# A 16-row, 512-byte write to the output ahead of all else in an interleaving copy

## Chip, cores and metric

The kernel runs on one core of a Trainium2 chip. The metric is the device time of one execution in microseconds (us); lower is better. Before the change three runs gave a median of 317.45 us (317.14 to 317.56). A difference counts as faster or slower here when it is over 2%, which is 6.3 us.

A ratio in this text is the mean time of one kernel's runs over the mean time of the other's runs of the same rounds. It is not quite the ratio of the medians that stand beside it.

## The reference

Two float32 arrays of 32 x 256 x 1024 (33.5 MB each) are interleaved element by element.

```python
def reference(x, y):
    batch, seq, dim = x.shape
    result = np.zeros((batch, seq, dim * 2), dtype=np.float32)
    result[..., 0::2] = x
    result[..., 1::2] = y
    return result.astype(np.float32)
```

Nothing is computed. 67.1 MB have to come in and 67.1 MB have to go out.

## The kernel before

The arrays are cut into eight blocks of 128 rows x 8192 elements. Loads are issued from the sync engine (the profile calls their queue q1). The vector engine (DVE) copies x to the even and y to the odd places of an output tile, in two halves for each block. Stores are issued from the scalar engine (queue q10). All tiles have two buffers.

```python
    WL = 8192
    WS = 4096
    ...
    xpool = ctx.enter_context(tc.tile_pool(name="xp", bufs=2))
    ypool = ctx.enter_context(tc.tile_pool(name="yp", bufs=2))
    opool = ctx.enter_context(tc.tile_pool(name="op", bufs=2))
    ...
    for lw in lwidths:                       # eight blocks
        ...
        nc.sync.dma_start(out=xtile, in_=xs)
        nc.sync.dma_start(out=ytile, in_=ys)
        soff = 0
        while soff < lw:                     # two halves
            ...
            nc.vector.tensor_copy(out=otile[:, 0::2], in_=xsub)
            nc.vector.tensor_copy(out=otile[:, 1::2], in_=ysub)
            nc.scalar.dma_start(out=os_, in_=otile)
            soff += width
        start += P * lw
```

## Time and profile before

| what | value | where it is read |
|---|---|---|
| time, median of 3 | 317.45 us | runs |
| span of the profiled execution | 315.0 us | first line of the page |
| last packet ends | 313.79 us | packet records of the trace |

A load or store of 4 MB is cut into 128 packets of 32 KB, eight for each of the 16 DMA engines. A packet normally takes 1.213 us. The prediction shows the lines of the page and how they are read.

### The profile page before, as it was taken

The numbers are of one execution on the slowest core, as the hardware profiler recorded it, in microseconds if no ns is written. First come the engines' busy times: TensorE is split into PE (matmuls) and PEld (weight loads), VectorE is DVE, ScalarE is ACT, GpSimd is POOL, SyncE is SP. The second block draws the span as 40 slices with busy tenths as digits, with TensorE's granted clock in tenths as the row PEclk, the third lists the DMA queues.
The fourth block names the chain that finished last, engine by engine and source line by source line (L and its number), as shares of the span: only waits on it lengthen the run. The fifth ranks groups of instructions, "written<-read, shape, count | busy, mean of one in ns | idle before, by whom it ended". The sixth has DMA issues, their size and how long they took to land.

```text
span 315.0 us, 148 instructions
## 1 busy us (share of the span) xinstructions
DVE 72.6 (23%) x32; POOL 0.2 (0%) x4
## 2 busy tenths in 40 slices
DVE  0334002214022230322204131040410505005500
POOL 0000000000000000000000000000000000000000
DMA  8999999999999999999999999999999999999997
GB/s 333 408 458 387 412 454 412 454 412 454 412 454 412 458 408 458 408 458 408 458 408 458 424 441 424 441 429 437 429 437 429 437 429 437 433 433 437 429 437 304
DMA packets 4608, 134.22 MB, mean 426 GB/s; under 512 B 512, under 2 KB 512, under 8 KB 512
## 3 DMA queue, kind: packets, MB, share of 16 engines
q1 hardware_dynamic: 2304, 67.11, 49.8%
q10 hardware_dynamic: 2304, 67.11, 49.3%
HBM read 67.11 MB, written 67.11 MB: 426 GB/s over the span
## 4 chain that ended last, share of the span: by engine, by line
DMA 83%; DVE 11%; DVEq 1%; issue 0%; SPq 0%
DMA out_dram<-otile 76%; DMA ytile<-in_y_dram 7%; DVE otile L64 6%; DVE otile L63 5%; DVEq L95 1%; SPq L49 0%; DVEq L63 0%
## 5 line engine op out<-in xcount | busy, mean ns | idle before, releaser
L63 DVE COPY otile<-xtile 128x4096 f32<-128x4096 f32 x16 | 36.6, 2294 | 197.9 <-DMA out_dram<-otile 184.8
L64 DVE COPY otile<-ytile 128x4096 f32<-128x4096 f32 x16 | 36.6, 2292 | 28.9 <-DMA ytile<-in_y_dram 28.9
L84 POOL MEMSET const-uint8-127<- 128x1 uint8 x1 | 0.1, 103 | 0.0
L84 POOL MEMSET const-bfloat16-1.0<- 128x1 bf16 x1 | 0.1, 102 | 0.0
L84 POOL MEMSET const-float32-1.0<- 128x1 f32 x1 | 0.1, 100 | 0.0
L84 POOL MEMSET const-float32-0.0<- 128x1 f32 x1 | 0.1, 99 | 0.2 <-issue 0.2
## 6 DMA issues: line engine op xcount, KB each, us to landing
out_dram<-otile ACTq DMA_DIRECT2D x16, 4096.0 KB, 30.6
xtile<-in_x_dram SPq DMA_DIRECT2D x8, 4096.0 KB, 42.1
ytile<-in_y_dram SPq DMA_DIRECT2D x8, 4096.0 KB, 59.2
```

Source lines behind the costliest of these rows:

```text
L63: nc.vector.tensor_copy(out=otile[:, 0::2], in_=xsub)
L64: nc.vector.tensor_copy(out=otile[:, 1::2], in_=ysub)
L84: nc = _bacc.Bacc("TRN2", target_bir_lowering=False, num_devices=1)
L95: with _tile.TileContext(nc) as tc:
```

## The change

The intent seems to be to make the first write to the output early, when nothing depends on it, so that whatever a first write costs is not paid in the middle of the stream. The bytes written are zeros. The first real store overwrites them, so the result stays right.

```diff
     assert sum(lwidths) == total // P
+
+
+    wpool = ctx.enter_context(tc.tile_pool(name="wp", bufs=1))
+    zero = wpool.tile([16, 128], fp32, name="zero")
+    nc.vector.memset(zero, 0.0)
+    first = dataclasses.replace(of, offset=0, ap=[[2 * WL, 16], [1, 128]])
+    nc.scalar.dma_start(out=first, in_=zero)
 
     start = 0
     for lw in lwidths:
```

## The prediction

> **What bounds the kernel now.** I read the page first: the busy shares, the row of GB/s in slices, the DMA queues and the chain that ended last.
>
> ```profile
> span 315.0 us, 148 instructions
> ...
> DVE 72.6 (23%) x32; POOL 0.2 (0%) x4
> ...
> DMA packets 4608, 134.22 MB, mean 426 GB/s; under 512 B 512, under 2 KB 512, under 8 KB 512
> ...
> q1 hardware_dynamic: 2304, 67.11, 49.8%
> q10 hardware_dynamic: 2304, 67.11, 49.3%
> ...
> DMA 83%; DVE 11%; DVEq 1%; issue 0%; SPq 0%
> ```
>
> The reader is to see three things. The only computing engine, the vector engine, works 23% of the span. The loads (q1) and the stores (q10) move 67.11 MB each, and their packets take 49.8% + 49.3% = 99.1% of the time of the 16 DMA engines, 0.991 x 315.0 = 312.2 us. And 83% of the chain is DMA. The 11% of DVE in the chain is not a bound: other transfers run under those copies, as the windows show. Their columns are start and end, length, busy time (and count) of DVE and of POOL, granted clock, DMA share, GB/s. I cut them at multiples of 14.55 us, twelve packets of 1.213 us, because the packets of the 16 engines run nearly in step and a shorter window shows that beat and not the rate.
>
> ```profile
> 0.00:1.70 1.70, 0.00 (x0) 0.20 (x4) 1.00 0.00 0
> 1.70:16.25 14.55, 3.17 (x2) 0.00 (x0) 1.00 1.04 430
> 16.25:30.80 14.55, 5.82 (x3) 0.00 (x0) 1.00 0.98 399
> 30.80:45.35 14.55, 0.00 (x0) 0.00 (x0) 1.00 1.00 432
> ...
> 74.45:292.70 218.25, 50.03 (x22) 0.00 (x0) 1.00 1.01 434
> 292.70:307.25 14.55, 4.50 (x2) 0.00 (x0) 1.00 1.01 437
> ```
>
> Nothing moves for 1.70 us. From 30.8 us to the end the rate is level at 432 to 437 GB/s whether the vector engine works or not. So the end is set by how many bytes there are, by the 1.7 us ahead of the first packet, and by whatever slows the engines on the way. One window stands out: 16.25 to 30.80 us, where the share is full (0.98) but the rate is 399.
>
> **The dip.** I looked at the single packet records of the trace. There are 4096 data packets of 32 KB, 256 for each engine, and nearly all take 1.213 us: 256 x 1.213 = 310.5 us. The first packet starts at 1.72 us and the last ends at 313.79 us, which is 312.07 us; the packet times sum to 312.02 us for an engine. So the engines have no gap worth naming. The 1.5 us over 310.5 are in two places only. The first packet of each of the 16 engines, which all start between 1.7 and 2.4 us, takes 1.3 to 2.2 us; over 1.213 this is 0.67 us for an engine. And 25 load packets that start between 26.6 and 30.5 us take 1.3 to 2.6 us, 0.82 us for an engine. Not one packet after that is longer than 1.26 us. This second place is where the first store arrives:
>
> ```profile
> 22.76 4.50 DVE L64 COPY otile<-ytile 128x4096 f32<-128x4096 f32 x2 [5.19 <-DMA ytile<-in_y_dram]
> 25.09 2.56 ACTq L65 DMA_DIRECT2D out_dram<-otile  x2
> 27.29 0.33 SPq L50 DMA_DIRECT2D ytile<-in_y_dram  x1
> ```
>
> In this stretch of the timeline the first two stores are issued at 25.09 us and some 2.2 us later. The first packet of q10 starts at 29.8 us; the loads just ahead of it are the stretched ones. So the kernel before pays 0.82 us once, when its store queue is used for the first time. The 16 to 30 us window agrees in size: (433 - 399) / 433 x 14.55 = 1.1 us, with part of that the edge of the window. A tiny write put ahead of everything looks meant for exactly this: to pay for the first write early. That is the whole prize there is.
>
> **What the Trainium skill says.** "DMA: Bandwidth & Descriptors", section "Where 436 GB/s comes from", gives a ceiling of 435.2 GB/s for the 16 ports. The trace agrees: 434 GB/s over 218 us. This leaves nothing to win in the steady part. The same page, "Queues, rings and completion order", says that each DMA engine takes turns between the queues that have work for it, a packet at a time. The trace fits: after 29.8 us packets of q10 and q1 alternate. So the small write can't be stuck behind the 8 MB of loads that are queued by then; it waits for a packet or two. The same page, "Two DMAs through the same engine are not ordered", says that order between two transfers comes only from waiting on the first one's semaphore. The first real store writes the same bytes, so a correct program must make it wait for the small write; the kernel before has no such wait. "Latency and other measured facts" gives 0.2 us on average and 2 us under high load for an access to HBM. The 0.67 us on each engine's first packet lies between; no record of the kernel before shows a small write by itself.
>
> **The change, part by part.** It removes nothing.
> - It adds a memset of 16 x 128 on the vector engine. This engine is idle until 13.08 us, and the four memsets of 128 x 1 on POOL take 0.10 us each. My estimate is 0.1 to 0.2 us near 0.7 us, in idle time. On the path to the end: 0.
> - It adds one issue on the scalar engine's queue, which idles until 25.09 us. The issues of stores take 0.34 us. On the path: 0, unless the loads' issues at 0.73 and 1.15 us are held up behind it. The small write has to wait for the memset, so the first load should go out first.
> - It adds 16 packets of 512 bytes and 16 semaphore packets, one pair for an engine. At 434 / 16 = 27.1 GB/s an engine moves 512 bytes in 0.02 us, and semaphore packets have 9 ns in the trace. Sum: some 0.03 us for an engine, on the path, since the engines have no gap: +0.03 us.
> - It adds a wait of the first store. If the small write is issued near 1 to 1.5 us and needs two packets' turns (2 x 1.2 to 2.2 us) and a round trip of up to 2 us, it lands by some 3 to 8 us. The first store can't go before 25.09 us. The wait costs 0. Later stores wrote other bytes, and in the kernel before the second store did not wait for the overlapping range of the first, so they gain no wait.
> - It moves every later transfer one place in the rotation of eight completion semaphores. A transfer that takes up a semaphore again waits for its last user; this was eight transfers, two rounds of the loop, before. One place more at the head leaves that distance at eight. Cost 0.
> - It may move the 0.82 us of the first write from 27 us to 2 us. There each engine sits in the 0.67 us of its first read anyway, so the two can overlap. If they overlap wholly the sum is 0.03 - 0.82 = -0.79 us; if not at all it is +0.03 us.
>
> **The rivals.** (A) The stall belongs to the first use of the store queue or of the way to the output, and the small write takes it in the shadow of the first reads: 317.45 - 0.3 to 0.8, so 316.6 to 317.1 us. For it: the stall is there once, and no packet after 32 us is stretched. (B) The stall belongs to a queue that wakes up while the other one keeps the engines full, or it is moved but not hidden. Then the small write has long drained by 25 us, the queue wakes up again, and the time stays at 317.4 to 317.6. For it: after the first two stores q10 never runs dry in the kernel before, so the trace can't tell "first" from "after idling". (C) The small write brings a stall of its own, in full, with the old one left where it is: +0.7 to 0.8, so 318.2 us. Against it: 512 bytes for an engine are little to stall on. (D) The first store's new wait takes the path: it would need the small write to land after 25.09 us, and q1's turns don't allow for that. An engine that becomes the bound I can't see: DVE would have to grow fourfold.
>
> **Range and chances.** I give A 0.45, B 0.4, C 0.15: 0.45 x 316.85 + 0.4 x 317.5 + 0.15 x 318.2 = 317.3; with the full prize possible in A I say 317.2 us. The three runs before spread over 0.42 us and the profiled run took 316.73, so I allow 0.4 beyond A's middle and stop just under C: 316.4 to 318.1 us. Two per cent are 6.3 us. The largest gain is 0.8 us, and even 1.72 us of start, 0.67 and 0.82 taken away together would be 3.2 us, 1%. No path to 2% is left upwards or downwards but a thing I have not seen: faster 0.01, same 0.98, slower 0.01.
>
> **What would show it.** Right: a span of 314.2 to 315.2 us, the same level 434 GB/s from 31 us on, 4640 packets, a DVE memset near 0.7 us, a small write that lands before 10 us, and the first store issued at 24 to 25.5 us without a new wait. A is right if the window 16.25 to 30.80 rises from 399 to over 420 and no load packet near 27 us is stretched; B if it stays near 400. Wrong: the first load's issue pushed past 1.2 us, a wait for the small write ahead of a store in the list of waits, or stretched packets later on.

## The result, and the profile after

The changed kernel took 316.34 us in the median (316.18 to 316.80, 6 runs). The kernel before took 317.13 us (316.34 to 317.56, 6 runs, with the three known ones among them). The ratio is 0.998, with a 95% interval of 0.9965 to 0.9995. This is the same within 2%, with a gain of about 0.2% that the interval sets apart from zero, though only just.

The page of the changed kernel, in the lines that answer to those of before:

```profile
span 314.5 us, 152 instructions
...
DVE 72.8 (23%) x33; POOL 0.2 (0%) x4
...
DMA packets 4640, 134.23 MB, mean 427 GB/s; under 512 B 528, under 2 KB 544, under 8 KB 544
...
q1 hardware_dynamic: 2304, 67.11, 49.9%
q10 hardware_dynamic: 2336, 67.12, 49.4%
...
out_dram<-zero ACTq DMA_DIRECT2D x1, 8.0 KB, 7.1
```

The reader is to see that q10 has 32 packets more, 16 of 512 bytes and 16 for semaphores, that the engines are as full as before, and that the 8 KB of the small write took 7.1 us from issue to landing. The timeline of the changed kernel shows where it lies:

```profile
0.73 0.37 SPq L56 DMA_DIRECT2D xtile<-in_x_dram  x1
0.81 0.17 DVE L45 MEMSET zero<- 16x128 f32 x1 [0.81 <-PEq L91]
1.01 0.42 ACTq L47 DMA_DIRECT2D out_dram<-zero  x1
1.15 0.42 SPq L57 DMA_DIRECT2D ytile<-in_y_dram  x1
...
25.01 33.63 ACTq L72 DMA_DIRECT2D out_dram<-otile  x3
```

Issued at 1.01 us, it landed at 8.1 us. The first store goes out at 25.01 us (25.09 before), so its new wait for the small write, over at 8.1 us, costs nothing. The loads are issued when they were before. The windows of the changed kernel, cut as those of before (start and end, length, busy time of DVE and POOL, clock, DMA share, GB/s):

```profile
1.70:16.25 14.55, 3.28 (x2) 0.00 (x0) 1.00 1.06 433
16.25:30.80 14.55, 5.72 (x3) 0.00 (x0) 1.00 0.96 396
30.80:45.35 14.55, 0.00 (x0) 0.00 (x0) 1.00 1.00 432
```

The dip at the first store is still there: 396 GB/s, against 399 before. So the small write did not take the hold-up away. The packet records say the same of the sum: near 27 us the stretched load packets cost 0.65 us for an engine, against 0.82 before. They also show a difference that the sum hides. Before, 14 engines start their first store packet between 29.82 and 30.35 us, and two only at 31.82 us, after a load packet of 2.6 us. After, all 16 start between 29.84 and 30.17 us, and no load packet there is longer than 1.95 us.

The records do not name the engine of a packet. It is found by following the times: each packet of an engine starts 3 to 4 ns before the one ahead of it ends. Followed in this way, the two engines run 23 loads ahead of their first store, and the other 14 run 22. In this text an engine with such a load more is called a late engine. That load only changed places with a store, so 1.21 us of the delay are not lost; the rest is, and the two end 0.65 us behind the middle engine.

The kernel ends with its slowest engine: in the twelve traces of the table that ends the experiments, the measured time is 2.90 to 2.94 us more than the end of the last packet. The last packet ended at 313.79 us before and at 313.34 us after, while the middle engine (the ninth of the 16 by the end of its last packet) ended at 313.14 and 313.22 us.

One trace each is no proof, so the experiments had two questions: is the gain real and is it these late engines, and what causes the general hold-up?

### The profile page after: what moved, and what is told of

Read it like the earlier page. It is cut to its first block, busy times and chain, and to the rows that moved or that the text cites. A ratio compares the mean times of both kernels' runs of the same rounds, so it can differ in the third digit from the quotient of the medians.

```text
span 314.5 us, 152 instructions
## 1 busy us (share of the span) xinstructions
DVE 72.8 (23%) x33; POOL 0.2 (0%) x4
## 4 chain that ended last, share of the span: by engine, by line
DMA 83%; DVE 11%; DVEq 1%; issue 0%; SPq 0%
DMA out_dram<-otile 76%; DMA ytile<-in_y_dram 7%; DVE otile L71 6%; DVE otile L70 5%; DVEq L102 1%; SPq L56 0%; DVEq L70 0%
## 5 line engine op out<-in xcount | busy, mean ns | idle before, releaser
L71 DVE COPY otile<-ytile 128x4096 f32<-128x4096 f32 x16 | 36.6, 2292 | 39.8 <-DMA ytile<-in_y_dram 39.8
```

## The experiments

Twelve runs were made, all with the right result. I name the theories as the expectations do. R: the difference is chance. W: the small write shortens the hold-up. V: each engine's first write to memory is slow now and then, and an early write takes that away. Q: it is the first use of queue q10. D: the general hold-up comes each time stores arrive at engines that were full of loads. F: that hold-up comes only once.

### 1. The changed kernel again (after_again)

No edit.

> The changed kernel unchanged, to see whether its 0.2% is there again and where it comes from. Theory R (the end is set by the engine that is held up longest at the first store, and that hold-up varies from execution to execution whatever the kernel): ratio to the kernel before between 0.998 and 1.002, with single times of both kernels spread over some 316.2 to 317.6 us; 16 to 30 load packets between 26 and 31 us stretched by 0.5 to 0.9 us for an engine, as in both traces so far. Theory W (the small write shortens the hold-up): ratio 0.997 to 0.999, interval below 1, and the stretch again at 0.65 us or under.

Measured: 316.54 us (316.38 to 316.78), the kernel before 316.73 us (316.19 to 317.56, 11 runs), ratio 0.999, interval 0.9975 to 1.0005. The hold-up was 0.94 us for an engine. By itself this doesn't confirm the gain, and W falls: the general hold-up is not shorter with the small write. But the kernel before had five of its 11 times between 317.2 and 317.6, and the changed kernel had none over 316.8.

### 2. The memset without the write (memset_only)

```diff
     nc.vector.memset(zero, 0.0)
-    first = dataclasses.replace(of, offset=0, ap=[[2 * WL, 16], [1, 128]])
-    nc.scalar.dma_start(out=first, in_=zero)
```

> The small write taken out of the changed kernel, its memset left in. Theory R: no difference to the kernel before, ratio 0.999 to 1.001, stretch near 27 us of 0.5 to 0.9 us for an engine. Theory W: as the kernel before, 1.000, with a stretch at about 0.82 us, and slower than the changed kernel of the same rounds by about 0.5 us. If it is as fast as the changed kernel and both are faster than before, the gain is not of the write.

Measured: 317.17 us (316.14 to 317.60), ratio 1.0005. Four of six times are above 317.0. In its trace one engine is late: its first store packet starts at 32.33 us, after a load packet of 3.03 us and one load more. Its windows from 312.5 us on show what that does to the end:

```profile
312.50:313.00 0.50, 0.00 (x0) 0.00 (x0) 1.00 0.00 0
313.00:313.40 0.40, 0.00 (x0) 0.00 (x0) 1.00 0.21 82
313.40:313.80 0.40, 0.00 (x0) 0.00 (x0) 1.00 0.00 0
```

The view counts a packet's bytes where the packet starts. 82 GB/s x 0.40 us is 32.8 KB: one single packet starts after 313.00 us, when all other engines have started their last one. It is the late engine's. It ends at 314.30 us, and the next slowest engine ended at 313.61 us. The same stretch of the changed kernel has no packet left to start:

```profile
312.50:313.00 0.50, 0.00 (x0) 0.00 (x0) 1.00 0.00 0
313.00:313.40 0.40, 0.00 (x0) 0.00 (x0) 1.00 0.02 0
313.40:313.80 0.40, 0.00 (x0) 0.00 (x0) 1.00 0.00 0
```

This points to the write, and not to the memset or the shifted program.

### 3. A larger early write (z_8k)

```diff
-    zero = wpool.tile([16, 128], fp32, name="zero")
+    zero = wpool.tile([16, 2048], fp32, name="zero")
     nc.vector.memset(zero, 0.0)
-    first = dataclasses.replace(of, offset=0, ap=[[2 * WL, 16], [1, 128]])
+    first = dataclasses.replace(of, offset=0, ap=[[2 * WL, 16], [1, 2048]])
```

> The early write 16 times as large for each row (8192 bytes, one packet for each engine), the memset 16 times as long. If the hold-up at the first store is a cost of the first write of some size, it should show at about 6 to 9 us as stretched load packets (0.5 us or more for an engine) and be gone near 27 us. If it belongs to the arrival of a long run of packets on an idle queue, near 27 us stays at 0.5 to 0.9 us. Time: 8192 bytes for an engine at 27 GB/s are 0.30 us, so about 0.3 us over the changed kernel in either case; a memset of 2 to 2.5 us in idle time costs nothing.

Measured: 316.85 us (316.60 to 317.24), 0.31 us over the changed kernel of the same rounds. Its larger packets (0.309 us each against 0.027) account for 0.28 us of that. Near 7 us only two load packets are longer than 1.23 us, the longest 1.37 us; near 27 us the hold-up is 0.91 us for an engine. So 8 KB from each engine do not bring the general hold-up forward. The whole kernel is shifted by some 0.4 us (first store packets from 30.23 to 31.14 us), with a longest load packet of 2.23 us. No engine has a load more ahead of its first store, but the one that starts its first store at 31.14 us (the next does so at 30.66) ends the kernel at 314.32 us, 0.60 us behind the middle engine. Two of the six times are above 317.0 (317.23 and 317.24); less the 0.31 us they would be at most 316.93.

### 4. Eight small packets for each engine (z_128rows)

```diff
-    zero = wpool.tile([16, 128], fp32, name="zero")
+    zero = wpool.tile([128, 128], fp32, name="zero")
     nc.vector.memset(zero, 0.0)
-    first = dataclasses.replace(of, offset=0, ap=[[2 * WL, 16], [1, 128]])
+    first = dataclasses.replace(of, offset=0, ap=[[2 * WL, 128], [1, 128]])
```

> The early write with 128 rows of 512 bytes instead of 16, so eight small packets for each engine instead of one. This sizes the term put at 0.03 us: each small packet took 27 ns in the changed kernel's trace, so 8 take 0.22 us and the time should be 0.19 us over the changed kernel of the same rounds, hardly to be told from the spread. Should each small packet cost a turn or a round trip of its own, it would be 1 us or more over. The stretch near 27 us stays if the queue's waking is its cause.

Measured: 316.45 us (316.34 to 316.80), which is 0.09 us under the changed kernel of the same rounds and not 0.19 us over it. The cost of small packets can't be told from the spread; it is not 1 us. Each took 27 ns in the trace. No engine is late.

### 5. A small load in place of the small write (touch_load, touch_load_again)

```diff
-    first = dataclasses.replace(of, offset=0, ap=[[2 * WL, 16], [1, 128]])
-    nc.scalar.dma_start(out=first, in_=zero)
+    first = dataclasses.replace(xf, offset=0, ap=[[WL, 16], [1, 128]])
+    nc.scalar.dma_start(out=zero, in_=first)
```

> In place of the small write, a small load of 16 rows of 512 bytes, on the same queue (q10) at the same moment. So far: without the small write 13 of 23 single times are above 317.0 us and in both traces one or two engines start their first store packet about 2 us after the others (31.8 to 32.3 us instead of 30), behind a load packet of 2.6 to 3.0 us; with a small write of 512-byte rows 0 of 18 times are above 317.0 and no engine is late. Theory Q (each engine's first use of q10 is slow now and then, and any early use takes that away): the load does as well as the write, no time above 317.0, no late engine, ratio 0.998 to 0.999. Theory V (it is the first write to the output or to memory that is slow): the load does nothing, half the times above 317.0, a late engine in the trace more often than not, ratio about 1.000.

> The small load instead of the small write, a second time, since one trace and five times decide little. Theory V: late engines as in its first trace and some times above 317.0 us, ratio 0.9995 to 1.0005. If there is no late engine and no time above 317.0 this time, its first trace was chance, and the load helps as well as the write.

Measured: 316.52 us (316.28 to 317.25), ratio 0.9996, and the second time 316.52 us (316.29 to 317.73), ratio 0.9993. In the first trace two engines start their first store packet at 31.54 and 31.65 us; in the second one engine starts at 32.20 us, behind a load packet of 2.50 us. In both traces these are late engines, with 23 loads ahead of the first store, so both speak for V. But in the first the two end at 313.51 and 313.62 us, where the slowest of the others ends at 313.59 us: there the late start cost next to nothing, and the execution took 316.52 us. The times alone don't decide: two of 11 are above 317.0, fewer than I expected of V. That the load helps a little is left open.

The second trace is of the slowest of these executions, 317.73 us. Its windows, from 312.5 us on:

```profile
312.50:313.00 0.50, 0.00 (x0) 0.00 (x0) 1.00 0.15 66
313.00:313.40 0.40, 0.00 (x0) 0.00 (x0) 1.00 0.02 0
313.40:313.80 0.40, 0.00 (x0) 0.00 (x0) 1.00 0.19 82
```

66 GB/s x 0.50 us and 82 GB/s x 0.40 us are 33 KB each: two single packets, of two engines. The first is the late engine's. It ends at 314.17 us, and the middle engine ended at 313.22 us. The second ends at 314.80 us and sets the time, but it is another engine's. That one started its first store at 30.83 us, with no load more, and has five load packets of 1.26 to 1.59 us later on, at 49, 54, 69, 71 and 246 us, 0.78 us in sum. In the other eleven traces of the table below no packet after 33 us is longer than 1.23 us. What held this engine up no run shows. By an estimate from the 2.93 us between last packet and time in this trace, the late engine alone would have given 317.1 us.

### 6. The small write on the queue of the loads (z_on_load_queue)

```diff
-    nc.scalar.dma_start(out=first, in_=zero)
+    nc.sync.dma_start(out=first, in_=zero)
```

> The same small write on the queue of the loads (q1), so between the first load and the second. Theory Q: q10 is as fresh as before when the first store comes, so half the times again above 317.0, plus what the later issue of the second load may cost (some 0.05 us). Theory V: the first write is made early, as in the changed kernel: no time above 317.0 and no late engine near 30 us.

Measured: 316.50 us (316.25 to 316.62), ratio 0.9989, interval 0.9977 to 1.0001. No engine is late (first store packets from 29.95 to 30.54 us), and no time is above 317.0, although q10 was fresh when the first store came. Five times alone would not decide, since the kernel before has only three of 11 above 317.0 in these rounds; with the trace, Q falls and V holds. The queue of the early write doesn't matter. That the early packet has to be a write rests on the two traces of the small load, each with a late engine.

### 7. One output buffer (out_bufs_1)

```diff
-    opool = ctx.enter_context(tc.tile_pool(name="op", bufs=2))
+    opool = ctx.enter_context(tc.tile_pool(name="op", bufs=1))
```

> The kernel before with one output buffer instead of two, so that a store can only be issued when the one ahead has landed, and q10 runs dry 15 times. The general hold-up of 0.6 to 0.8 us for an engine, which the small write did not remove, then tells its cause. Theory D (it comes each time a run of store packets arrives at engines that were full of loads): stretched load packets ahead of each of the first stores, not of the first alone, as long as loads still fill the engines. Theory F (once only, at the first large store): stretched packets near 27 us alone. Time: the loads then are held up by the copies and by single stores, so slower in any case, 5 to 30%.

Measured: 372.07 us, ratio 1.1734, as a kernel that has to wait for each store. The records answer the question. The table has stretches of its trace of 2.426 us each (two packets), with the packets that start in them and what the stretched ones cost for an engine.

| from, us | loads | stores | stretched beyond 1.23 us | cost for an engine | longest packet |
|---|---|---|---|---|---|
| 26.7 | 28 | 0 | 24 loads | 0.80 us | 3.27 us |
| 36.4 | 16 | 16 | none | 0 | 1.21 us |
| 58.2 | 17 | 7 | 17 loads | 0.61 us | 2.02 us |
| 63.1 | 16 | 16 | none | 0 | 1.21 us |
| 104.3 | 17 | 12 | 17 loads | 0.63 us | 2.06 us |
| 150.4 | 15 | 16 | 15 loads | 0.61 us | 2.03 us |

Each time stores come back to engines that have been running loads alone, each engine is held up by about 0.6 us, on the last load ahead. The three later returns, at 197, 243 and 288 us, show 0.55 to 0.60 us. While both kinds take turns there is nothing, and when stores come back to engines that have run out of loads (from 86.5 us on) no packet is more than 0.04 us over its time either. Where the loads run out just as stores come back, some store packets take up to 2.04 us, 0.07 to 0.25 us for an engine (near 177, 222, 268 and 313 us). (Loads that start on idle engines take longer too, 0.62 us for an engine from 53.4 us on, as the first loads of every kernel here do.) D holds and F falls. In the windows of this kernel such a return is a stretch with a full DMA share and a low rate, followed by the full rate:

```profile
104.30:106.70 2.40, 0.00 (x0) 0.00 (x0) 1.00 1.05 341
106.70:116.40 9.70, 0.00 (x0) 0.00 (x0) 1.00 1.01 436
```

And the late engine is another matter than this hold-up: two engines with 23 loads, and load packets of 3.01 and 3.27 us, are there at the first store only. At the six later returns no load packet is over 2.20 us.

### 8. The loads of y on the store queue (y_on_store_queue)

```diff
-        nc.sync.dma_start(out=ytile, in_=ys)
+        nc.scalar.dma_start(out=ytile, in_=ys)
```

> The kernel before with the loads of y issued on the store queue, so that q10 is busy with loads from the start and the first store arrives at a queue that is running. Theory Q: no late engine at the first store and no slow mode, but perhaps a late engine at the start. Theory D: no hold-up at the first store, since both queues already take turns; 0.6 us less, 316.0 us, if nothing else is lost. Against that: the stores stand behind loads in one queue, and loads of y stand behind stores that wait for the copies, which may open gaps later; 316 to 330 us.

Measured: 319.62 us (319.04 to 322.02), ratio 1.0099. I had expected no hold-up at the first store under D, since both queues take turns from the start. It was there all the same: 27 packets between 39.8 and 41.9 us, 0.76 us for an engine, when the first store had got through q10 behind the loads. It had been issued at 27.15 us, so the hold-up goes with the packets of the store and not with its issue. In the windows:

```profile
19.40:38.80 19.40, 8.90 (x4) 0.00 (x0) 1.00 1.01 434
38.80:43.65 4.85, 0.00 (x0) 0.00 (x0) 1.00 1.08 399
43.65:58.20 14.55, 0.00 (x0) 0.00 (x0) 1.00 1.00 432
```

So D has to be worded more narrowly. By this one trace it is not a queue that wakes up, but engines with loads alone that get their first stores. Later in the run there are three more such stretches (1.42 us for an engine from 77 to 84 us, 0.50 us from 157 to 165 us, 0.48 us from 236 to 242 us). The four sum to 3.16 us, 2.3 us more than the 0.82 us of the kernel before. The traced execution took 319.04 us, which is 2.3 us over the kernel before of these rounds (316.78 us). What arrives at which engine in the later ones I have not sorted out.

### 9. The kernel before again (before_again)

No edit.

> The kernel before against itself, for the size of a difference that means nothing, and for one more trace. Ratio 0.999 to 1.001. If one or two engines are late at the first store more often than not, its trace shows a first store packet at 31.5 us or later and a load packet of 2.6 us or longer just ahead, as both traces without an early write to memory did, and as the one with a small load did (31.5 and 31.6 us); some of its times, or of the other runs of the kernel before, are then above 317.0 us.

Measured: 316.68 us (316.35 to 317.15), against 317.06 us (316.28 to 317.55) for the same kernel in the other runs of these rounds, ratio 0.9994. So a ratio within 0.001 of one means nothing here. In this trace no engine was late (first store packets from 29.84 to 30.28 us) and the time was 316.39 us. I had expected a late one. A late engine is not certain in this kernel, and this execution without one was as fast as the changed kernel.

### 10. The changed kernel a third time (after_third)

No edit.

> The changed kernel a third time, beside the kernel before on the same chip. Theory V (the first write of each engine to memory is slow now and then, and the early write takes that away): no late engine (all first store packets between 29.8 and 30.8 us), no time above 317.0 us, ratio 0.9985 to 0.9995. Theory R (chance): a late engine or times above 317.0 as often as in the kernel before.

Measured: 316.38 us (316.13 to 316.55), the kernel before 317.06 us, ratio 0.9982, interval 0.9971 to 0.9994. No engine is late and no time is above 317.0, as V expected; the ratio is a little under its 0.9985.

### 11. The small write somewhere else (z_far)

```diff
-    first = dataclasses.replace(of, offset=0, ap=[[2 * WL, 16], [1, 128]])
+    first = dataclasses.replace(of, offset=2 * total - 2 * P * WL, ap=[[2 * WL, 16], [1, 128]])
```

> The small write goes to rows of the last block of the output, 58 MB further on, instead of the rows that the first store writes; the first store then has no wait for it, the second last store has. If what matters is a first write of each engine to memory, wherever: as the changed kernel, no late engine and no time above 317.0 us. If the bytes near the first store's must have been touched: late engines and times as in the kernel before. The wait of the first store that is gone was worth nothing, so no gain from that.

Measured: 316.31 us (316.24 to 316.83), ratio 0.9984, interval 0.9972 to 0.9997. No engine is late. The bytes that the first store writes need not be touched; a write to rows 58.7 MB further on does the same. The first store has no wait for the small write here, and that is worth nothing.

### All traces and times together

The columns are: how many engines are late (23 loads ahead of the first store), when the 16 engines start their first store packet, the longest load packet near it, the hold-up for an engine (the mean over 16), and the end of the last packet of the middle and of the slowest engine.

| kernel | early write | late engines | first store packets, us | longest load, us | hold-up, us | middle and last end, us |
|---|---|---|---|---|---|---|
| before | no | 2 | 29.82 to 31.82 | 2.63 | 0.82 | 313.14, 313.79 |
| before_again | no | 0 | 29.84 to 30.28 | 1.97 | 0.73 | 313.19, 313.46 |
| memset_only | no | 1 | 29.83 to 32.33 | 3.03 | 0.87 | 313.24, 314.30 |
| touch_load | no (load) | 2 | 29.91 to 31.65 | 2.18 | 0.82 | 313.28, 313.62 |
| touch_load_again | no (load) | 1 | 29.83 to 32.20 | 2.50 | 0.85 | 313.22, 314.80 |
| after | yes | 0 | 29.84 to 30.17 | 1.95 | 0.65 | 313.22, 313.34 |
| after_again | yes | 0 | 29.97 to 30.70 | 2.23 | 0.94 | 313.38, 313.88 |
| after_third | yes | 0 | 30.03 to 30.48 | 2.16 | 0.86 | 313.34, 313.65 |
| z_128rows | yes | 0 | 29.87 to 30.25 | 1.92 | 0.63 | 313.27, 313.42 |
| z_far | yes | 0 | 29.81 to 30.22 | 2.07 | 0.79 | 313.17, 313.40 |
| z_on_load_queue | yes | 0 | 29.95 to 30.54 | 2.22 | 0.90 | 313.32, 313.72 |
| z_8k | yes, 8 KB rows | 0 | 30.23 to 31.14 | 2.23 | 0.91 | 313.72, 314.32 |

The hold-up is the same with and without the early write: its mean is 0.82 us in the first five rows and 0.80 us in the six with a small write of 512-byte rows. What differs are the late engines: four of the first five traces have them, and so has out_bufs_1, but none of the seven traces with an early write. The slowest engine ends 0.78 us behind the middle one in the mean of the first five rows and 0.29 us in the mean of the six. Of the 0.78 us, 0.13 us come from the other engine of touch_load_again.

The single times agree. Without an early write or load there are 51 (the kernel before 45 times in all, memset_only six times): mean 316.86 us, lowest 316.14, 23 of them above 317.0. With a small write of 512-byte rows there are 33: mean 316.46 us, lowest 316.13, highest 316.83, none above 317.0. The difference of 0.40 us is 0.13% and comes nearly all of the slow executions: without the 23 the first mean is 316.53 us, and the lowest times are equal. R falls: with 45% of times above 317.0, 33 in a row without one would be no chance. The limit of 317.0 was first named when 41 of these times were known. Of the later ones, 10 of 28 of the kernel before are above it, and none of 15 with a small write. The times are pooled over several chips, so I lean on the missing slow times and not on the second digit of the mean.

So it is shown that the small write takes away the slow executions. That late engines are what makes them slow is less firm. A time above 317.0 us needs a last packet that ends after some 314.1 us. Only two of the kept traces without an early write are of such executions, memset_only and touch_load_again. Both have a late engine that ends past that (314.30 and 314.17 us). But in the kernel before and in touch_load the late engines ended at 313.8 and 313.6 us, so not every late engine makes a slow execution.

## Why the prediction was right or wrong

**The class and the bound were right.** No path to 2% was open, and the DMA engines stayed the bound. The span was put at 314.2 to 315.2 us and is 314.5 us.

**The number was a little high.** I said 317.2 us with a range from 316.4 us. The median was 316.34 us, just under that range, and 316.54 and 316.38 us in the two repeats, around its low end. Most of the gap is the starting point. I took 317.45 us as the kernel's time, but those three runs fell in its upper part: over 45 times its mean is 316.83 us. The ratio of 0.998, put on 317.45, gives 316.8 us.

**The costs added were right.** The memset took 0.17 us in idle time (0.1 to 0.2 said). The issue took 0.42 us and did not delay the loads. A small packet took 0.027 us and its semaphore packet 0.009 us, so 0.036 us for an engine against 0.03. No new wait of a load or a store shows up in the list of waits, so the rotation of semaphores did nothing that can be seen.

**The landing was put too early, without effect.** I let the small write wait for two packets' turns. The records show it behind three load packets on each engine, starting at 6.1 to 6.5 us, and it landed at 8.1 us, just past the 3 to 8 us. The first store needed it at 25 us.

**The step that failed is "it may move the 0.82 us of the first write from 27 us to 2 us".** I took the 0.82 us as one cost, paid once, at the first use of the store queue. The runs showed two costs in it. One is a hold-up of each engine by 0.6 to 0.9 us, which comes back each time stores arrive at engines that carry loads alone, which no small early write takes away, and which needs no fresh queue. That is close to rival B, but B's reason, the waking queue, fell with y_on_store_queue. The other is a late engine or two at the first large write after none, in some executions. It can set the end, because the kernel ends with its slowest engine: in memset_only it ended at 314.30 us, 0.69 us behind the next. No trace with an early write has one, and the gain is that the executions above 317.0 us are gone (23 of 51 times without a small write, none of 33 with one). I had the packets of it before me (two loads of 2.6 us among 25 stretched ones) and averaged them over 16 engines, where two of them count for little. Where all must finish, the slowest counts and not the mean.

So rival A was right that an early write helps, but for a part of the stall that I had not set apart. That the 0.40 us lie in its 0.3 to 0.8 is luck: that range was worked out from the 0.82 us, which stayed. My own test of A against B, the 16.25 to 30.80 us window, came out for B (396 GB/s, "near 400"), while B's time was wrong. C and D of the prediction fell: no stall came with the small write, and its wait is off the path.

**What stays open.** What inside a DMA engine is slow at its first write, and why only one or two engines are hit, no run shows. Nor do the runs settle whether an early load helps as well in part: with it 2 of 11 times are above 317.0, between 23 of 51 and none of 33. The same holds for why loads are held up when stores arrive. In y_on_store_queue, which has no early write, no load packet at the first store was over 1.96 us; one trace can't say whether the late engine is gone there or was absent by chance.

No run beat the changed kernel by more than the spread, so there is no better version to offer. z_far and z_on_load_queue are equal to it.

## What to carry to other kernels

When 16 DMA engines share one stream evenly, look at the engine that finishes last and at its longest packets before averaging a dip over all; and look at the spread of single times, since a change may cut the slow executions and leave the fast ones as they were. A tiny early write got the first write over with at no cost that could be measured, but it was worth only 0.13% here. In out_bufs_1, which switches between loads alone and loads with stores many times, each return of the stores cost about 0.6 us for each engine; the kernels that keep both kinds running paid it once.

## What the Trainium skill lacked or had wrong

- "DMA: Bandwidth & Descriptors", section "Queues, rings and completion order", says that an engine takes turns between the queues it has work for, a packet at a time, and puts a packet at some 9 to 17 descriptors. While both queues have work, the traces show turns of one 32 KB packet of the records (16 of each kind start in 2.426 us); how many descriptors such a packet holds they don't show. The page doesn't say how long a queue that was empty waits for its first turn: the small write, issued at 1.01 us, came after three whole load packets on each engine (at 6.1 to 6.5 us), and the first store, issued at 25.01 us, from 29.84 us on.
- The same page lacks the hold-up when stores reach engines that run loads alone: 0.6 to 0.9 us for an engine, at each such return (0.61, 0.63 and 0.61 us in out_bufs_1), and also when the store's queue was busy with loads (0.76 us in y_on_store_queue).
- No page has the late engine at the first large write to memory: in five of the six traces without an early write that load from one queue, one or two engines ran 23 loads ahead of their first store where the others ran 22, with a load packet of 1.95 to 3.27 us, and in none of the seven traces with an early write.
